# A bidirectional encoder layer on one core: the convolution is woven in denser, the backward states start among the last key sweeps, and eight instead of five steps of the recurrence stand beside the memory products

## The chip, the cores and the metric

The kernel runs on one core of a Trainium2 chip. The metric is the device time of one execution in microseconds. The time of the kernel before is the median of three runs.

## The reference, cut to what matters

One layer works on `x` of 2048 rows by 1024 columns and on 256 memory rows. A combined projection feeds two halves: a gated long convolution over 512 channels, done by transforms, and a recurrence with 4 heads in two directions (the mLSTM). Their outputs are joined and projected. A cross-attention into the memory and a feed-forward part follow.

```
u = rms_norm(x);  proj = u @ w_in                      # 1024 -> 3600 columns
hy = short_conv(proj[:, :1536])                        # z, g1, g2 of 512 columns each
for o, gate in enumerate((g1, g2)):                    # the convolution, order 2
    z = gate * (irfft(rfft(z, 2L) * spec[:, o])[:L] + z * skip[o])
q, k = silu(short_conv(proj[:, 1536:2560]));  v, o_pre, gates = proj[:, 2560:]
h = scan(q, k, v, gates[forward]) + flip(scan(flip(q), flip(k), flip(v), flip(gates[backward])))
y_ml = sigmoid(o_pre) * h                              # each scan: states C, n carried from chunk to chunk
x = x + concat(norm(z), norm(y_ml)) @ w_out
x = x + softmax(rms_norm(x) @ wq @ (memn @ wk).T) @ (memn @ wv) @ wo
x = x + relu(rms_norm(x) @ w1) ** 2 @ w2;  out = rms_norm(x)
```

## The kernel before, in words

All arithmetic is in 32-bit floats. The large products are split in a high and a low half, and each is three products of halves (lines 355, 358, 359 in `mm3`); an operand is split by a copy on ScalarE and a subtraction on VectorE (line 366).

The parts are written as Python generators. Each `yield` is a place where another part may put its instructions, and the number yielded is the weight of the step that follows. `weave(a, b, wa, wb)` advances whichever of two generators is behind in the ratio `wa` to `wb`; `among(g, h, n)` lets `h` take one step after every n-th step of `g`, and what is left of `h` at the end; `beside_each(g, h)` alternates one step of each, and `take(g, n)` hands on n steps. A scheduler then sets the final order of each engine's instructions, from this order of writing and from its own model of durations. Each engine works through its list in that order. SyncE issues most transfers and GpSimd the stores, also in order.

The parts that the change touches, by their methods of `Prog`:

- `sweep(cols, hf, first)`: a quarter of the projection's transposed columns for one half (1024) of the rows. Column pairs 0 to 5 are the convolution's three inputs, 6 and 7 are q, 8 and 9 are k. Each step is 24 products of 128x512 (`mm<-xh,wh` and so on), weight 5.5.
- `natural(hf, tiles)`: the projection's untransposed columns: tiles 0 and 1 are v, 2 and 3 the output gate, and tile 3 also the gates' columns. Each step is 4 x 24 products of 128x256 (`mm<-wh,xh`), weight 11.
- `hyena`: the convolution. For each of two orders it has three stages. The *spectrum* takes 8 blocks of z into frequency space (lines 173 and 186 with `f` as the second operand; the result is stored to `zs`). The *middle* goes over 16 blocks of frequencies (lines 956, 1030 and 987; it loads `zs` and stores `zg`). The *return* goes over 8 blocks (lines 173 and 186 with `e` as the second operand; it loads `zg`, multiplies by the gate at line 1051, and in order 1 normalises and stores `yh`). In order 0 a return block is followed by the spectrum of the next order's block.
- `gates`: small scans of the recurrence's gates over all chunks, on VectorE, with a few transposes on TensorE (lines 1093, 1134, 1149, 1171).
- `states` (through `backward` and `update`): the backward direction's state after each of chunks 15 down to 1: load `kn` and `va`, scale `va` on GpSimd (line 1196), 4 products (line 1200), 4 operations on VectorE (line 1206), store to `cbd`.
- `memproj`: the memory products. Eight weights (4 heads of keys, 4 of values): `project` (line 708), then `keys` (line 725) or `values` (line 737), each result copied by ScalarE to one of three `o` buffers (line 715) and stored by GpSimd to `gd` or `vw`.
- `mlstm`: the recurrence's outputs, 16 chunks of 128 rows. The first step loads chunks 0 and 1 and makes the scores of chunk 0. Then one step for each chunk n: scores of chunk n+1 (line 1284; exponentials on ScalarE at 1293, masks on GpSimd at 1291), outputs of chunk n in both directions (lines 1322 and 1324; the backward one reads `cbn`, loaded from `cbd`), the forward state's update (line 1200 with `ve`), and after every second chunk a normalisation (`bank_rsqrt`, lines 205 to 217, and line 1356). The scores, outputs and updates share four PSUM banks, `hy`, with the convolution.
- `attention`: the joined projection (line 1479 transposes `yh` and `ym`, products `mm<-act,wh`), then cross-attention; the remaining steps of `mlstm` are woven into it.

`program` holds the order of the whole. Its middle, as quoted below, writes in turn: the rest of the sweeps with the convolution woven in at 445 to 329; `gates` among a sweep of columns 4, 5, 8, 9 for the first half of the rows; `states` among the last natural tiles and the sweep of columns 6 and 7; then one step of `memproj`, and from there one step of `memproj` and one of `mlstm` in turn until five steps of `mlstm` (its loads, then chunks 0 to 3) are written; then `attention`.

Of the kernel before, what the change touches and what calls it, by code (L numbers as in the profile page):

```python
# [2076 lines left out]
def chain(*gens):  # L2077
    for g in gens:
        yield from g


def weave(a, b, wa, wb, until=False):
    da = db = 0.0
    fa = fb = False
    while not (fa and fb):
        if fb or (not fa and da / wa <= db / wb):
            try:
                da += next(a)
            except StopIteration:
                fa = True  # L2090
        else:
            try:
                db += next(b)
            except StopIteration:
                fb = True
                if until:
                    return


def program(p):  # L2100
    with ExitStack() as ms:
        with ExitStack() as es:
            p.inproj_open(es)
            p.filters_open()
            p.prepq = p.x_first()
            p.pop()
            s = chain(p.sweep(range(4), 0, True, lambda: p.prep_x(1)), p.opened(), p.sweep(range(4), 1, False))
            f = p.filters()
            for _ in range(5):
                next(s)  # L2110
            next(f)
            next(f)
            next(s)
            weave(s, f, 140, 102, True)
            p.gates_open(es)
            n = p.memproj()
            m = p.mlstm(ms)
            with ExitStack() as hs:
                rest = chain(s, p.sweep(range(4, 10), 1, True), p.natural(1, (3, 0, 1, 2), True),
                             p.natural(0, (3,)), among(p.sweep((4, 5, 8, 9), 0, False), p.gates(), 2),  # L2120
                             among(chain(p.natural(0, (0, 1)), p.sweep((6, 7), 0, False),
                                         p.natural(0, (2,), p.prep_mem, 2)), p.states(), 1),
                             )
                weave(rest, p.hyena(hs), 445, 329)
            for _ in chain(p.turned_in(), take(n, 1), beside_each(n, take(m, 5))):
                pass
        with ExitStack() as rs:
            p.ts = rs.enter_context(ExitStack())
            p.tail_open(p.ts)
            with ExitStack() as at:  # L2130
                g = p.attention(at)
                weave(g, m, 440, 112, True)
                ms.close()
                p.ffn_open(rs)
                for _ in g:
                    pass
            p.ffn()


def among(g, h, every):  # L2140
    for i, v in enumerate(g):
        yield v
        if i % every == every - 1:
            next(h, None)
    for _ in h:
        pass


def beside_each(g, h):
    for v in g:  # L2150
        yield v
        yield next(h, 0)
    yield from h


def take(g, n):
    for _ in range(n):
        v = next(g, None)
        if v is None:
            return  # L2160
        yield v
# [31 lines left out]
```

## Time and profile before

| | |
|---|---|
| median of the runs | 3072.69 us (3072.32 to 3078.89) |
| the profiled execution, its own time | 3076.22 us |
| its span, first to last instruction | 3074.5 us |
| TensorE (PE) busy | 2984.5 us, 97% |
| VectorE (DVE), ScalarE (ACT), GpSimd (POOL) busy | 1938.8, 1493.0, 1259.7 us |
| mean granted TensorE clock | 0.987 |
| moved by DMA | 607.03 MB, 197 GB/s |

TensorE (PE) is the engine to watch: where it is busy at full clock, other engines' waits cost nothing. Time can only be won where it stands idle or runs at a lower granted clock. Matmul records overlap (they are pipelined), so the time that a run of products takes is read from start to start. A product written once in the code stands as two records in the profile for plain 32-bit operands (lines 173, 186, 708, 725, 737, 956, 1030, 1200, 1284, 1322 and 1324), and as one for the split halves (355, 358, 359) and for transposes (825, 1479).

### The profile page before, as it was taken

To read this page: it belongs to the slowest core of one execution; us is meant where nothing else is said; L and a number is where in the kernel's file an instruction comes from. 1 tells how busy PE (TensorE), PEld (TensorE's weight loads), DVE (VectorE), ACT (ScalarE), POOL (GpSimd) and SP (SyncE) were. 2 spreads that over 40 slices of the span, in tenths; PEclk is the share of its full clock that TensorE was granted. 3 is DMA by queue.
4 is the path that set the end of the run, shared out by engine and by line. 5 is a ranking of instruction groups with operands and counts; after the bars stand their busy time and mean duration, and the time that the engine had idled before them with its cause. 6 is when DMAs were issued, how large, how long until landed. Compare 5 with 4: busy or idle time off the path is not lost.

```text
span 3074.5 us, 44129 instructions
## 1 busy us (share of the span) xinstructions
PE 2984.5 (97%) x14799; PEld 2369.8 (77%) x14799; DVE 1938.8 (63%) x3442; ACT 1493.0 (49%) x2930; POOL 1259.7 (41%) x1025
## 2 busy tenths in 40 slices
PE   9999999998999988999999999999999999999998
PEld 7666667775678757888887888888888888888876
DVE  7855454657656347867665665557555676566695
ACT  6443455635654236555544455556555543333335
POOL 0112123411344654333133247765566374344653
PEclk9999999999999988999999999999999999999999
DMA  6655687596877965464567466657544565344434
GB/s 219 196 188 171 214 271 219 184 297 200 258 223 249 349 231 192 158 220 131 188 203 259 147 210 216 208 181 243 186 154 151 195 198 171 118 158 120 155 103 164
DMA packets 423643, 607.03 MB, mean 197 GB/s; under 512 B 36846, under 2 KB 229998, under 8 KB 422392
## 3 DMA queue, kind: packets, MB, share of 16 engines
q1 hardware_dynamic: 395972, 525.42, 53.3%
q0 software_dynamic: 18992, 62.96, 5.6%
q10 hardware_dynamic: 8452, 15.83, 1.4%
q8 instruction: 117, 1.92, 0.3%
q14 instruction: 110, 0.90, 0.1%
HBM read 401.67 MB, written 202.41 MB: 196 GB/s over the span
## 4 chain that ended last, share of the span: by engine, by line
PE 58%; DVE 2%; DMA 1%; issue 1%; ACT 0%; POOL 0%; SPq 0%; DVEq 0%; ACTq 0%; POOLq 0%
PE mm L355 12%; PE mm L359 12%; PE mm L358 12%; PE hy L355 6%; PE hy L359 6%; PE hy L358 6%; PE hy L1322 1%; PE hy L1324 1%; DVE bl L1693 0%; PE hy L1284 0%; PE hy L1479 0%; PE hy L1596 0%; DVE acc L1991 0%; PE hy L1200 0%; DVE acc L2028 0%
## 5 line engine op out<-in xcount | busy, mean ns | idle before, releaser
L1692 ACT CAST ah<-w 128x512 fp32r<-128x512 f32 x284 | 176.7, 623 | 304.0 <-PE hy L358 157.8
L1693 DVE TENSOR_TENSOR bl<-wr,bh 128x512 fp32r<-128x512 f32 x213 | 235.5, 1110 | 131.1 <-ACT bh L1692 131.0
L366 DVE TENSOR_TENSOR wl<-wn,wh 128x512 fp32r<-128x512 f32 (+1 forms) x296 | 216.6, 775 | 94.3 <-ACT wh L366 94.3
L355 PE MATMUL mm<-xh,wh 128*128 128x512 f32 x640 | 263.3, 413 | 3.7 <-ACT wh L366 1.2
L358 PE MATMUL mm<-xl,wh 128*128 128x512 f32 x640 | 254.1, 397 | 4.5 <-DVE xl L366 4.4
L1692 ACT CAST bh<-wr 128x512 fp32r<-128x512 f32 x232 | 143.4, 621 | 229.0 <-PE mm L359 177.5
L359 PE MATMUL mm<-xh,wl 128*128 128x512 f32 x640 | 253.7, 397 | 0.0
L1693 DVE TENSOR_TENSOR al<-w,ah 128x512 fp32r<-128x512 f32 x236 | 213.6, 905 | 55.7 <-ACT ah L1692 55.6
L359 PE MATMUL mm<-bh,al 128*128 128x512 f32 x576 | 223.7, 391 | 4.0 <-DVE al L1693 4.0
L355 PE MATMUL mm<-bh,ah 128*128 128x512 f32 x576 | 225.8, 392 | 0.1
L358 PE MATMUL mm<-bl,ah 128*128 128x512 f32 x576 | 224.9, 390 | 0.0
L366 ACT CAST wh<-wn 128x512 fp32r<-128x512 f32 (+1 forms) x296 | 164.4, 620 | 105.8 <-PE mm L359 51.0
L358 PE MATMUL mm<-act,wh 128*128 128x512 f32 x512 | 202.0, 394 | 0.0
L355 PE MATMUL mm<-act,wh 128*128 128x512 f32 x512 | 199.4, 396 | 2.0 <-ACT wh L366 1.9
L359 PE MATMUL mm<-act,wl 128*128 128x512 f32 x512 | 199.9, 392 | 0.0
L355 PE MATMUL hy<-bh,ah 128*128 128x512 f32 x448 | 175.2, 391 | 0.0
L358 PE MATMUL hy<-bl,ah 128*128 128x512 f32 x448 | 174.6, 390 | 0.0
L359 PE MATMUL hy<-bh,al 128*128 128x512 f32 x448 | 174.4, 390 | 0.0
L331 POOL TENSOR_TENSOR b<-b 128x512 f32<-128x512 f32 x32 | 48.1, 1505 | 294.6 <-DVE b L330 275.2
L355 PEld LDWEIGHTS mm<-xh,wh 128*128 128x128 f32 x640 | 120.5, 188 | 53.1 <-issue 19.4
L358 PEld LDWEIGHTS mm<-xl,wh 128*128 128x128 f32 x640 | 120.6, 188 | 49.2 <-issue 18.6
L355 PE MATMUL mm<-wh,xh 128*128 128x256 f32 (+1 forms) x512 | 154.7, 302 | 0.0
(396 smaller groups left out, 8262.9 us busy)
## 6 DMA issues: line engine op xcount, KB each, us to landing
wr<-hc SPq DMA_DIRECT2D x224, 256.0 KB
w<-in_ff_w_dram SPq DMA_DIRECT2D x172, 256.0 KB
hc<-wn SPq DMA_DIRECT2D x128, 256.0 KB
wn<-in_w_in_dram SPq DMA_DIRECT2D x100, 256.0 KB
hc<-q SPq DMA_DIRECT2D x96, 256.0 KB
fs<-a SPq DMA_DIRECT2D x32, 512.0 KB
zs<-a POOLq DMA_DIRECT2D x32, 512.0 KB, 6.0
a<-fs SPq DMA_DIRECT2D x64, 256.0 KB
```

What stands on the lines that cost most here:

```text
L331: nc.gpsimd.tensor_tensor(b, f, b, ALU.subtract)
L355: first = mm(ps, lh, rh, start=start, stop=False)
L358: mm(ps, lh, rl, start=False, stop=False)
L359: self.last = mm(ps, ll, rh, start=False, stop=stop)
L366: both = (self.nc.scalar.copy(hi, src), self.nc.vector.tensor_tensor(lo, src, hi.bitcast(F32), ALU.subtract))
L1322: nc.tensor.matmul(dst, nm[:, h], va[:, h], start=True, stop=state is None)
L1324: nc.tensor.matmul(dst, rows_[d, 1][:, h], state[:, h], start=False, stop=True)
L1692: self.nc.scalar.copy(hi, src)
L1693: eng.tensor_tensor(lo, src, hi.bitcast(F32), ALU.subtract)
```

## The change

The order in `program` is changed; no instruction's work is.

```
-                             p.natural(0, (3,)), among(p.sweep((4, 5, 8, 9), 0, False), p.gates(), 2),
-                             among(chain(p.natural(0, (0, 1)), p.sweep((6, 7), 0, False),
-                                         p.natural(0, (2,), p.prep_mem, 2)), p.states(), 1),
+                             p.natural(0, (3,)),
+                             paced(chain(p.sweep((4, 5, 8, 9), 0, False), p.natural(0, (0, 1))),
+                                   p.gates(), back := p.states(), (0, 1) * 6 + (2,) * 6 + (2, 0)),
+                             among(chain(p.sweep((6, 7), 0, False), p.natural(0, (2,), p.prep_mem, 2)), back, 1),
                              )
-                weave(rest, p.hyena(hs), 445, 329)
-            for _ in chain(p.turned_in(), take(n, 1), beside_each(n, take(m, 5))):
+                weave(rest, p.hyena(hs), 400, 329)
+            for _ in chain(p.turned_in(), take(n, 1), beside_each(n, take(m, 8))):
                 pass
+def paced(g, h1, h2, plan):
+    for v, n in zip(g, plan):
+        yield v
+        if n:
+            next((h1, h2)[n - 1], None)
+    yield from g
```

- The weave of projection and convolution goes from 445:329 to 400:329, so that the convolution advances faster against the projection and is written to its end when the projection has some 45 units of weight left.
- `paced` takes the steps of `gates` after every second one of the first 12 steps of the sweep of columns 4, 5, 8 and 9, as before, and then 7 steps of `states` after the sweep's last four steps and the first three of the v tiles. Before, `states` began with the v tiles. The rest of `states` goes among the sweep of columns 6 and 7 and the last output-gate tile.
- Eight steps of `mlstm` (the loads, then chunks 0 to 6) are written beside the memory products and right after them, where five were.

How the scheduler then placed things, at three places. First TensorE's list at the end of the memory products, before. L708 and L737 are memory products, L173 and L186 with `e` the convolution's return, L1284 scores of the recurrence, L1322 and L1324 its outputs.

```order
L708 MATMUL mm<-mt,wm 128x256 x6
L173 MATMUL hy<-a,e_2743 32x512
L186 MATMUL hy<-a,e_2743 32x512 x7
L708 MATMUL mm<-mt,wm 128x256 x10
L737 MATMUL mm<-wm,kt 128x512 x10
L1284 MATMUL hy<-qn,kk_t 128x128 x8
L737 MATMUL mm<-wm,kt 128x512 x6
L1322 MATMUL hy<-va,rw 128x129 x5
L1324 MATMUL hy<-cbn,rw 128x129
```

And the place in the changed kernel where the recurrence's first chunk begins; L725 is a memory product of the keys, L1200 with `va` a backward state.

```order
L725 MATMUL mm<-kt,wm 128x256 x16
L1200 MATMUL hy<-va,kn 128x129 x8
L708 MATMUL mm<-mt,wm 128x256 x7
L1284 MATMUL hy<-qn,kk_t 128x128 x8
L708 MATMUL mm<-mt,wm 128x256 x9
L725 MATMUL mm<-kt,wm 128x256
L1322 MATMUL hy<-va,rw 128x129 x6
L725 MATMUL mm<-kt,wm 128x256 x12
L1324 MATMUL hy<-cbn,rw 128x129
```

Before, the last memory product stands ahead of the first output of chunk 0, and the scores of chunk 0 and 1 stand six products ahead of it. Now 57 products of line 708, 16 of line 725 and 32 of line 737 stand behind those scores, and outputs of chunks 0 to 4 stand among them. The last two backward states stand seven products ahead of the scores.

Second, TensorE's list at the end of the memory products in the changed kernel (the scores here are those of chunk 6, the outputs those of chunk 5):

```order
L737 MATMUL mm<-wm,kt 128x512 x3
L1200 MATMUL hy<-ve,kn 128x129 x4
L737 MATMUL mm<-wm,kt 128x512 x3
L1284 MATMUL hy<-qn,kk_t 128x128 x4
L1322 MATMUL hy<-va,rw 128x129
L1324 MATMUL hy<-cf,rw 128x129
L1322 MATMUL hy<-va,rw 128x129
```

Behind the last memory product stand the outputs of chunks 5 and 6 (16 products each) with their updates, and then 16 transposes of line 1479. Before, it was the outputs of chunks 0 to 3, and then the same transposes.

Third, TensorE's list where order 1 of the convolution goes from the spectrum to the middle. Before, 24 sweep products, 4 transposes (L825) and small ones stand between the last spectrum block (L173, L186 with `f`) and the first product of the middle on it (L1030); this is the end of that piece:

```order
L355 MATMUL mm<-xh,wh 128x512
L358 MATMUL mm<-xl,wh 128x512
L359 MATMUL mm<-xh,wl 128x512
L825 MATMUL mm<-ident,cv 128x128 x4
L1030 MATMUL hy<-a,dm 128x512 x2
```

Now 9 sweep products and the pair of line 956 stand there:

```order
L186 MATMUL hy<-a,f_104 64x512 x7
L355 MATMUL mm<-xh,wh 128x512
L358 MATMUL mm<-xl,wh 128x512
L359 MATMUL mm<-xh,wl 128x512
L355 MATMUL mm<-xh,wh 128x512
L358 MATMUL mm<-xl,wh 128x512
L359 MATMUL mm<-xh,wl 128x512
L355 MATMUL mm<-xh,wh 128x512
L358 MATMUL mm<-xl,wh 128x512
L359 MATMUL mm<-xh,wl 128x512
L956 MATMUL mm<-a,dm 128x512 x2
L1030 MATMUL hy<-a,dm 128x512 x2
```

So the first product on the last spectrum block moved nearer to it. The transposes of `gates` (L1093, L1134, L1149, L1171) moved too: before they stand among the return and spectrum blocks of order 0, now all of them stand in the middle of order 1.

On TensorE's list two return blocks of order 1 stand among the memory products now, where six stood, and five updates of `states` stand there, where six stood. On SyncE's list the first loads of the joined projection's weights now stand ahead of twelve transfers of memory weights, and their first waits for the convolution's last stores; before, the first load with such a wait (`wn<-yh`) stood behind the last memory weight.

## The prediction, made before the changed kernel had run

> **What bounds the kernel now.** I read the page first, then the busy time by stretches, then TensorE's timeline where it is idle, then the waits.
>
> ```profile
> PE 2984.5 (97%) x14799; PEld 2369.8 (77%) x14799; DVE 1938.8 (63%) x3442; ACT 1493.0 (49%) x2930; POOL 1259.7 (41%) x1025
> ...
> PE   9999999998999988999999999999999999999998
> ...
> PEclk9999999999999988999999999999999999999999
> ```
>
> TensorE (PE) is busy for 97% of the span, so only 90 us of idle time and some time at a low clock can be had at all. The change adds no work to PE. What it can move is where PE waits.
>
> The stretches of 75 us show where (columns: busy time of PE, PEld, DVE, ACT, POOL; granted clock; DMA share; GB/s):
>
> ```profile
> 675.00:750.00 75.00, 64.67 (x370) 41.35 (x369) 55.14 (x173) 32.73 (x57) 9.46 (x15) 0.93 0.70 231
> ...
> 975.00:1050.00 75.00, 72.69 (x427) 61.38 (x426) 34.62 (x102) 21.14 (x51) 47.15 (x56) 0.98 1.02 347
> ...
> 1125.00:1200.00 75.00, 54.27 (x309) 49.07 (x310) 49.79 (x165) 40.78 (x156) 32.66 (x29) 0.80 0.63 208
> 1200.00:1275.00 75.00, 75.00 (x392) 64.15 (x392) 61.74 (x155) 44.59 (x129) 30.65 (x24) 1.00 0.50 155
> ```
>
> The worst stretch, 1125 to 1200 us, has 20.7 us of idle time and a clock of 0.80. It is the place that the last part of the change is about. The second worst, 675 to 750 us, is the return of order 0 with `gates` on top. In the next stretch PE is full, with the recurrence woven into the attention.
>
> PE's timeline through the worst stretch:
>
> ```profile
> 1116.84 5.32 PE L737 MATMUL mm<-wm,kt 128*128 128x512 f32 x12
> 1121.99 1.28 PE L1322 MATMUL hy<-va,rw 128*128 128x129 f32 x10
> ...
> 1126.80 1.16 PE L1284 MATMUL hy<-qn,kk_t 128*128 128x128 f32 x8
> 1127.80 0.39 PE L1322 MATMUL hy<-va,rw 128*128 128x129 f32 x2
> 1128.02 0.39 PE L1324 MATMUL hy<-cf,rw 128*128 128x129 f32 x2
> ...
> 1135.22 0.67 PE L1322 MATMUL hy<-va,rw 128*128 128x129 f32 x2 [4.58 <-DVE den L1330]
> ...
> 1139.83 1.16 PE L1284 MATMUL hy<-qn,kk_t 128*128 128x128 f32 x8 [0.93 <-DVE cf L1206]
> ...
> 1158.80 1.92 PE L1284 MATMUL hy<-qn,kk_t 128*128 128x128 f32 x8
> ...
> 1165.63 1.23 PE L1200 MATMUL hy<-ve,kn 128*128 128x129 f32 x8 [0.36 <-ACT ht L1336]
> ...
> 1174.90 1.12 PE L1479 MATMUL hy<-ident,wn 128*128 128x128 f32 x4 [5.17 <-DVE act L366]
> ...
> 1179.10 1.49 PE L355 MATMUL mm<-act,wh 128*128 128x512 f32 x4
> ...
> 1194.11 1.91 PE L1479 MATMUL hy<-ident,wn 128*128 128x128 f32 x16
> ```
> ```profile
> 1140.00:1150.00 10.00, 4.92 (x25) 4.49 (x26) 6.58 (x22) 4.12 (x20) 1.73 (x2) 0.61 0.40 109
> 1150.00:1160.00 10.00, 7.07 (x30) 6.48 (x31) 7.87 (x31) 4.74 (x18) 7.31 (x7) 0.50 0.28 105
> ```
>
> The last memory product's run ends at 1121.99. From there to the first product of the joined projection at 1179.10, PE has only the recurrence: outputs of chunks 0 to 3, one chunk waiting for the other through ScalarE, VectorE and GpSimd. I call such chunks bare. That is 57.1 us, part of it at half clock, as the two stretches of 10 us show.
>
> **Term 1, the bare chunks.** A chunk's content at full clock: scores 1.0 us (1126.80 to 1127.80), outputs 16 products at 0.22 us (a row of two records follows the other after 0.22), 3.6 us, update about 1.0: 5.6 us. In the 57.1 us there are 64 output products (12 + 3 x 16 + 4: 14.3 us), four updates (4), four scores (4) and the 16 transposes (1.9, as at 1194.11): 24.2 us. So 32.9 us are lost. In the changed list two chunks are bare, 5 and 6: 36 output products (8.1), two updates, three scores and the transposes: 15 us. How long they take I read from the old ones. From scores to scores, or to the update's end, chunk 1 took 13.0 us (1126.80 to 1139.83), chunk 2, behind the normalisation of the pair before, 19.0 (to 1158.80), chunk 3 8.1 (to 1166.86). Chunk 5 is like 1 and 3, taken as 10; chunk 6 is like 2, taken as 17, since the clock was already halved when chunk 2 began. The tail from there to the first product was 12.2 us; 5.2 of it is a wait for VectorE, busy with a normalisation that will not stand there (the next comes after chunk 7), so 8. That gives 35 us instead of 57.1: 22.1 us shorter, of which 9.2 is content that goes elsewhere. Gain 12.9, between 3.7 (13, 19 and 12.2: 44.2 us) and 17.8 (8.1, 15 and 7: 30.1 us).
>
> **Term 2, the chunks beside the memory.** The moved content costs what it costs; the question is waits. Prices of the memory products and the waits among them now:
>
> ```profile
> 1041.74 5.45 PE L725 MATMUL mm<-kt,wm 128*128 128x256 f32 x24
> ...
> 1047.02 7.07 PE L708 MATMUL mm<-mt,wm 128*128 128x256 f32 x32
> ...
> 1106.47 8.75 PE L737 MATMUL mm<-wm,kt 128*128 128x512 f32 x20
> ```
> ```profile
> 1011.66 3.03 PE L725 MATMUL mm<-kt,wm 128*128 128x256 f32 x8 [2.31 <-ACT kt L710]
> 1086.33 1.16 PE L1200 MATMUL hy<-va,kn 128*128 128x129 f32 x8 [2.94 <-POOL va L1196]
> ```
>
> The waits among them are 5.3 us. A product of line 708 or 725 takes 0.44 us, one of 737 0.875. So from scores to scores the list now gives chunks 1 to 4 18.6, 14.6, 19.4 and 14.2 us (their own 5.6 and 9, 14 and 10 memory products or the like). Against their own pace of 8 to 19 us that is just enough for odd ones, and short by a little for chunk 4 and its like. I take 4 us of waits over the four chunks (0 where the pace at full clock is shorter, 12 where each waits 3). Chunk 0 needs the last backward state: store to `cbd`, then load `cbn`.
>
> ```profile
> L1206 DVE SCALAR_TENSOR_TENSOR cb<-cb,cols,hy x56: 336/342/352, 872.1 to 1087.9; 128x129 f32<-128x129 f32 x56
> ```
> ```profile
> cbd<-cb POOLq DMA_DIRECT2D x6, 258.0 KB, 7.9
> ```
>
> From the last two updates, which stand together: eight operations of VectorE 2.7, 7.9 from issue to landing (the median over 985 to 1125 us), a load of 3.4 like that of `zs` under term 3: 14.0 us. The list has 7 products, 8 scores, 9 + 1 products and 4 outputs in between: 17 x 0.44 + 1.9 + 0.9 = 10.3. So a wait of 3.7, less if the transfers are lighter loaded. Six return blocks leave this stretch with their loads, where the DMA share is 1.02 now; that relieves it. Sum 7.7 against 5.3: a loss of 2.4 (bounds: a gain of 3, a loss of 12).
>
> **Term 3, the denser convolution.** The price of sweep products and of the pair of line 956, and the passage from spectrum to middle of order 1 before:
>
> ```profile
> 406.99 0.39 PE L358 MATMUL mm<-xl,wh 128*128 128x512 f32 x1
> 407.22 0.40 PE L359 MATMUL mm<-xh,wl 128*128 128x512 f32 x1
> 407.45 1.88 PE L956 MATMUL mm<-a,dm 128*128 128x512 f32 x4
> ...
> 728.88 0.63 PE L186 MATMUL hy<-a,f 32*64 32x512 f32 x7
> ...
> 731.04 1.05 POOL L339 DMA_DIRECT2D zs<-a  x2 [2.47 <-ACT st L201]
> ...
> 736.26 1.16 SPq L920 DMA_DIRECT2D a<-zs  x2
> ...
> 739.70 2.90 PE L1030 MATMUL hy<-a,dm 128*128 128x512 f32 x3 [3.62 <-DMA a<-zs]
> ```
>
> From the last block's end at 729.5 it takes 10.2 us through GpSimd, a store and a load, and 3.6 of it is a wait. The cover goes from 24 sweep products and transposes to 9 products at 0.23 (2.1) and the pair of line 956 (1.9): 4.0 us. The wait becomes 6.2, a loss of 2.6. The list also has spectrum and return blocks back to back at three places, where the banks have to be copied out first; I take 0.5 each, 1.5 (0 to 5.4, at the 1.81 of the row at 714.81 below). In return, `gates` leaves order 0's return, where PE waits:
>
> ```profile
> 705.97 0.64 PE L173 MATMUL hy<-a,f 32*64 32x512 f32 x1 [1.30 <-DVE a L1051]
> 712.62 0.37 PE L1134 MATMUL hy<-ident,ends 128*1 128x128 f32 x1 [2.70 <-DVE ends L1129]
> 714.81 1.03 PE L173 MATMUL hy<-a,e 64*32 64x512 f32 x1 [1.81 <-issue]
> ```
>
> These 5.8 us go, but the same scans now load VectorE in the middle of order 1. I keep 4 of them: gain 1.8. Sum: a loss of 2.3 (bounds: a gain of 3, where the new place hides the scans and the blocks cost nothing; a loss of 9, where it hides none and VectorE's 5.8 us come a second time).
>
> The attention loses three chunks from its cover; PE was full in 1200 to 1275 us with them, so nothing. `states` starts four sweep steps earlier; its products waited for no one there, nothing.
>
> **Sum.** -12.9 + 2.4 + 2.3 = -8.2 us. The profiled execution took 3076.22 us (span 3074.5), 3.5 above the median of the runs; from it 3068.0 would follow, from the median, against which the result is measured, 3064.5.
>
> The Trainium skill, "TensorE: Matmul & The Clock Gate", section "HAM oscillation — how this bites in real kernels", says that an idle gap of TensorE of more than about 3.4 us halves its clock. The trace agrees: rows of line 1322 take 0.39 us before the wait of 4.58 and 0.67 behind it. By this rule the waits of 3.7 and 6.2 above would each be followed by a window at half clock, an estimate of 1.7 us each from the page's figure; the sum would be -4.8, 3067.9 us.
>
> **Rivals.**
>
> A is the forecast: two bare chunks less, part of it given back in waits. 3060 to 3070.
>
> B: the chunks beside the memory wait for nothing new (the store of `cbd` lands in time, because the transfers are relieved), and the denser convolution costs nothing net. For it speaks that in 1200 to 1275 us such chunks cause no idle time at all; against it, that they have far more cover there. -12.9 - 3 + 0 = -15.9, 3056.8.
>
> C: the denser convolution takes the gain back. Where VectorE is late in the middle of order 1, PE waits at each of its 16 blocks; at the bound of 9 us, with term 2 as above, it is -1.5: 3071.2.
>
> D, slower: ScalarE's queue. The copies of memory results (line 715) wait there for one of three buffers, until its store has landed:
>
> ```profile
> ACT o L715 <- DMA gd<-o: 27.6, 9, 8.5
> ...
> ACT o L715 <- DMA vw<-o: 7.2, 3, 4.2
> ```
>
> That is 34.8 us in which ScalarE's list stands still. It costs little now, because next to nothing of the recurrence stands behind them. In the changed list the exponentials, output scalings and update scalings of chunks 0 to 6 do. If half of it reaches PE, 17.4 us come on top: +9.2, 3081.9. Against it speaks that fewer other transfers compete, so stores land sooner. It decides the sign when more than 8.2 of the 34.8 us reach PE. The Trainium skill, "TensorE: Matmul & The Clock Gate", section "Architectural detail: the array is 16× 32×32, not 1× 128×128", calls ScalarE's and VectorE's queues strictly first in, first out; that is the rule by which nothing could overtake such a copy.
>
> **How the numbers follow.** A 0.40, B 0.25, C 0.18, D 0.17. About 0.2%, 6 us, is what a measurement of this kernel tells from no change. A lies across that bound and counts 0.25 as faster, 0.15 as the same; B is faster, C the same, D slower but for 0.02. Faster 0.50, same 0.35, slower 0.15. The range 3051 to 3079 holds A, C, nearly all of B and the milder cases of D, some 0.85.
>
> **What would show it.** Right: between the last memory product and the first product of the joined projection some 35 us instead of 57; a clock near 0.9 over those 75 us; outputs of chunk 0 to 4 among the memory products with one wait of 3 to 6 us before the first backward output; a wait of about 6 us at line 1030 where order 1's middle starts. Wrong: waits of line 1322 for ScalarE among the memory products that add up to more than 10 us, or 715 waiting as long as now (D); line 1134 waiting over 5 us (C); the bare stretch still over 45 us, which would take away the gain.

## The result and the profile after

| | before | after |
|---|---|---|
| median of the runs | 3072.51 us (3071.01 to 3078.89) | 3090.55 us (3087.36 to 3097.53) |
| ratio to before, 95% interval | | 1.0058 (1.0035 to 1.0081) |
| the profiled execution, span | 3074.5 us | 3090.8 us |
| first memory product (line 708) | 988.1 us | 1033.2 us |
| first product of the joined projection | 1179.1 us | 1209.6 us |
| from there to the end | 1895.4 us | 1881.2 us |

The changed kernel is slower by about 18 us; 8 us less had been forecast. In the two spans the difference is 16.3 us: 45.1 us lost up to the first memory product, 14.6 won from there to the joined projection, 14.2 won behind it.

The page's lines for TensorE (PE), after:

```profile
PE 2984.9 (97%) x14799; PEld 2367.8 (77%) x14799; DVE 1954.6 (63%) x3442; ACT 1494.0 (48%) x2930; POOL 1263.6 (41%) x1025
...
PE   9999999988999998999999999999999999999998
...
PEclk9999999999999998999999999999999999999999
```

The work is the same. In the rows by tenths the dent behind the memory (slices 15 and 16 before) is down to slice 16, and the one in slice 10 (692 to 769 us before) now takes slices 9 and 10 (618 to 773 us). The stretches that the prediction showed, after (columns as there):

```profile
675.00:750.00 75.00, 64.24 (x327) 40.69 (x326) 36.73 (x63) 32.70 (x56) 13.84 (x17) 0.95 0.70 216
...
975.00:1050.00 75.00, 75.00 (x485) 63.94 (x484) 57.65 (x126) 30.32 (x53) 44.24 (x49) 1.00 0.81 259
...
1125.00:1200.00 75.00, 66.87 (x352) 50.57 (x351) 42.48 (x162) 37.74 (x144) 39.87 (x43) 0.96 0.67 223
1200.00:1275.00 75.00, 70.75 (x383) 61.88 (x382) 59.54 (x133) 44.59 (x129) 32.24 (x25) 0.93 0.62 195
```

1125 to 1200 us had 54.27 us of work at a clock of 0.80. That place is mended. Where the time went is seen in four stretches ahead of the memory, first before, then after:

```profile
340.00:400.00 60.00, 56.28 (x336) 39.86 (x333) 25.46 (x39) 27.25 (x41) 7.84 (x13) 1.00 0.86 298
400.00:530.00 130.00, 125.03 (x634) 89.49 (x634) 76.69 (x121) 82.35 (x142) 38.90 (x44) 0.99 0.72 229
600.00:750.00 150.00, 137.26 (x878) 98.55 (x877) 100.83 (x249) 63.92 (x111) 28.46 (x36) 0.97 0.76 245
750.00:900.00 150.00, 147.81 (x726) 104.53 (x725) 95.84 (x151) 99.44 (x174) 59.86 (x65) 1.00 0.77 237
```
```profile
340.00:400.00 60.00, 48.85 (x291) 32.43 (x291) 25.45 (x38) 26.84 (x41) 8.89 (x15) 0.89 0.87 284
400.00:530.00 130.00, 122.54 (x535) 83.54 (x534) 76.65 (x123) 81.52 (x139) 38.49 (x42) 0.99 0.74 231
600.00:750.00 150.00, 132.31 (x903) 96.96 (x902) 77.03 (x134) 59.23 (x105) 28.39 (x39) 0.98 0.81 252
750.00:900.00 150.00, 133.03 (x486) 82.89 (x486) 121.58 (x263) 99.87 (x168) 55.18 (x57) 0.95 0.71 217
```

PE's idle time grows by 7.4, 2.5, 5.0 and 14.8 us, 29.7 in all. In the two stretches whose clock fell, that costs another 0.11 x 60 + 0.05 x 150 = 14 us, as an estimate. Two places carry it: the convolution's first blocks (340 to 400), and the middle of its order 1 (750 to 900), where VectorE's busy time rises from 95.84 to 121.58 us.

At the first place PE's waits, before and then after, with one block that waits for nothing:

```profile
352.01 0.64 PE L173 MATMUL hy<-z,f 32*64 32x512 f32 x1 [1.10 <-ACT a L311]
...
360.08 0.61 PE L173 MATMUL hy<-z,f 32*64 32x512 f32 x1 [1.17 <-ACT a L998]
...
381.86 0.61 PE L173 MATMUL hy<-a,f 32*64 32x512 f32 x1 [1.45 <-DMA a<-hy]
```
```profile
346.57 0.64 PE L173 MATMUL hy<-z,f 32*64 32x512 f32 x1 [2.69 <-ACT a L311]
...
379.88 1.08 PE L173 MATMUL hy<-a,f 32*64 32x512 f32 x1 [4.73 <-DMA a<-hy]
...
389.03 0.64 PE L173 MATMUL hy<-a,f 32*64 32x512 f32 x1
...
389.51 0.63 PE L186 MATMUL hy<-a,f 32*64 32x512 f32 x7
...
393.84 0.64 PE L173 MATMUL hy<-a,f 32*64 32x512 f32 x1 [3.70 <-ACT a L998]
```

3.7 us of waits became 11.1. A block, 16 records, takes 1.1 us (389.03 to 390.14); behind the long wait a record of line 173 takes 1.08 instead of 0.64.

At the second place, the convolution's largest wait for VectorE, and VectorE's own list ahead of its end:

```profile
774.64 2.04 PE L956 MATMUL mm<-a,dm 128*128 128x512 f32 x2 [7.13 <-DVE a L960]
```
```profile
769.38 0.27 DVE L1114 TENSOR_TENSOR pad<-pad 64x128 f32<-64x128 f32 x1
769.69 0.29 DVE L1115 TENSOR_TENSOR pad<-pad 64x128 f32<-64x128 f32 x1
...
771.59 0.29 DVE L1115 TENSOR_TENSOR pad<-pad 64x128 f32<-64x128 f32 x1
...
772.27 0.69 DVE L1034 TENSOR_TENSOR b<-hy,a 128x512 f32<-128x512 f32 x1
772.99 0.69 DVE L959 COPY a<-mm 64x512 f32<-64x512 f32 x1
773.70 0.69 DVE L960 COPY a<-mm 64x512 f32<-64x512 f32 x1
```

The copy that frees the bank for line 956 (773.70) stands behind the doubling steps of `gates` (lines 1114 and 1115). VectorE works through its list in order and is busy for 19.48 of the 20 us from 770 to 790. The scans are not all that it does there: copies and products of the middle (lines 959, 960, 1034) stand among them.

Behind the memory, PE's timeline where the prediction priced chunks 5 and 6:

```profile
1176.95 2.74 PE L737 MATMUL mm<-wm,kt 128*128 128x512 f32 x6
1179.53 1.05 PE L1284 MATMUL hy<-qn,kk_t 128*128 128x128 f32 x8
...
1186.45 1.16 PE L1284 MATMUL hy<-qn,kk_t 128*128 128x128 f32 x8 [0.70 <-DVE cf L1206]
...
1195.71 0.77 PE L1322 MATMUL hy<-va,rw 128*128 128x129 f32 x2 [6.26 <-DVE bry L213]
1196.27 0.64 PE L1324 MATMUL hy<-cbn,rw 128*128 128x129 f32 x2
...
1204.67 3.35 PE L1479 MATMUL hy<-ident,wn 128*128 128x128 f32 x16
...
1209.57 0.71 PE L355 MATMUL mm<-act,wh 128*128 128x512 f32 x2
```

From the last memory product (1179.7) to the joined projection it is 29.9 us, where it was 56.9 with four bare chunks.

### The profile page after: what moved, and what is told of

Same layout as the page of the kernel before. It is cut to its first block, busy times and chain, and to the rows that moved or that the text cites. A ratio compares the mean times of both kernels' runs of the same rounds, so it can differ in the third digit from the quotient of the medians.

```text
span 3090.8 us, 44177 instructions
## 1 busy us (share of the span) xinstructions
PE 2984.9 (97%) x14799; PEld 2367.8 (77%) x14799; DVE 1954.6 (63%) x3442; ACT 1494.0 (48%) x2930; POOL 1263.6 (41%) x1025
## 4 chain that ended last, share of the span: by engine, by line
PE 54%; DVE 2%; DMA 2%; issue 1%; POOL 1%; ACT 0%; SPq 0%; DVEq 0%; ACTq 0%; POOLq 0%
PE mm L355 12%; PE mm L359 12%; PE mm L358 12%; PE hy L359 6%; PE hy L355 6%; PE hy L358 6%; DMA w<-in_ff_w_dram 1%; PE hy L1322 0%; PE hy L1324 0%; PE hy L1479 0%; DVE bl L1693 0%; DVE al L1693 0%; DMA h<-acc 0%; PE hy L1596 0%; DVE acc L1991 0%
## 5 line engine op out<-in xcount | busy, mean ns | idle before, releaser
L1522 POOL TENSOR_TENSOR ssum<-ssum,sq 128x512 f32<-128x512 f32 x56 | 81.2, 1450 | 200.9 <-ACT sq L1521 191.8
```

Of the source, the lines that this page charges most:

```text
L1522: nc.gpsimd.tensor_tensor(ssum, ssum, sq, ALU.add)
```

## The experiments

Fifteen kernels were run. The table puts them side by side: the ratio to before, the first memory product, the time from there to the joined projection, how much of that is the bare stretch (from the last memory product) with how many chunks wholly in it by TensorE's list, and the rest to the end. The last four columns are of the profiled execution, a single one, whose time lies up to 5 us beside the median of its kernel (e14 5.4 below, e19 4.6 above), so that a few us between two rows of them say little.

| kernel | ratio (95% interval) | first memory product, us | to the joined projection | bare stretch (chunks) | rest |
|---|---|---|---|---|---|
| before | 1 | 988.1 | 191.0 | 56.9 (4) | 1895.4 |
| after | 1.0058 (1.0035 to 1.0081) | 1033.2 | 176.4 | 29.9 (2) | 1881.2 |
| e1 ratio only | 1.0083 (1.0068 to 1.0099) | 1035.6 | 170.6 | 32.7 (2) | 1891.0 |
| e7 eight steps only | 1.0067 (1.0052 to 1.0083) | 989.3 | 224.0 | 93.3 (7) | 1875.4 |
| e10 earlier states only | 0.9969 (0.9958 to 0.9980) | 998.0 | 173.6 | 38.5 (2) | 1890.4 |
| e2 after, ratio undone | 1.0033 (1.0020 to 1.0045) | 998.7 | 209.1 | 76.5 (5) | 1874.2 |
| e14 after, five steps | 1.0026 (1.0014 to 1.0037) | 1030.4 | 152.1 | 11.1 (0) | 1889.1 |
| e3 after, scans cut | 1.0040 (1.0025 to 1.0055) | 1031.3 | 177.0 | 31.1 (2) | 1874.3 |
| e4 after, later start | 1.0027 (1.0014 to 1.0039) | 1008.7 | 191.7 | 55.2 (4) | 1874.3 |
| e21 e4 and old middle | 1.0068 (1.0054 to 1.0082) | 1004.5 | 213.8 | 71.6 (5) | 1873.2 |
| e23 e21, scans cut | 1.0054 (1.0040 to 1.0069) | 995.0 | 212.1 | 70.5 (5) | 1875.4 |
| e16 e10, scans later | 0.9983 (0.9971 to 0.9994) | 1001.3 | 172.2 | 38.6 (2) | 1889.0 |
| e11 e10, order 1 at 1/0.72 | 0.9998 (0.9985 to 1.0011) | 1015.3 | 163.4 | 23.6 (1) | 1889.9 |
| e12 e10, order 1 at 1/0.85 | 0.9959 (0.9946 to 0.9971) | 1001.2 | 160.8 | 25.9 (2) | 1890.8 |
| e19 e12, old passage | 0.9955 (0.9942 to 0.9969) | 1002.3 | 166.3 | 26.9 (2) | 1888.9 |
| e13 e10, closer return | 0.9972 (0.9961 to 0.9984) | 992.3 | 175.3 | 37.6 (2) | 1891.6 |
| e18 e13, weight ahead of the middle | 0.9982 (0.9973 to 0.9992) | 996.0 | 178.1 | 35.4 (2) | 1890.6 |

Behind the first memory product still stand 2 to 6 return blocks (1.1 us each) and 3 to 9 backward states (1.2 us each), by kernel; between two kernels that makes up to 6 us of content. A hundredth of a per cent of the ratio is 0.3 us.

**The three parts apart.** Theory T, after the traces were compared: the denser convolution costs what was lost ahead of the memory, and the other parts are innocent of it.

e1, on the kernel before:

```
-                weave(rest, p.hyena(hs), 445, 329)
+                weave(rest, p.hyena(hs), 400, 329)
```

> The kernel before with the ratio 400:329 alone. Theory T (the denser convolution itself costs the time: it starts earlier in the first sweeps, its blocks stand back to back, and the gates' scans fall beside order 1's middle): the first memory product starts 35 to 45 us later than before, the bare stretch behind the memory shortens by 10 to 20 us (some five chunks, two or three of them bare), and the time is 3085 to 3100 us. Rival T3 (the earlier backward states cost it): the way to the first memory product loses under 15 us, and the time is 3050 to 3070.

3098.12 us: the first memory product 47.5 us late, bare stretch 24.2 us shorter. T holds, though both lie above its ranges (35 to 45 and 10 to 20), and T3 falls.

e2, on the changed kernel:

```
-                weave(rest, p.hyena(hs), 400, 329)
+                weave(rest, p.hyena(hs), 445, 329)
```

> The changed kernel with the ratio back at 445:329, so that earlier states and eight steps of the recurrence stay. Theory T: the way to the first memory product is as long as before within 6 us, and four or five chunks are bare again at some 8 us of loss each, so 3070 to 3085 us. Rival T3 (the earlier states): at least 20 of the 39 us on the way to the memory stay lost, and the time is 3090 to 3110.

3081.89 us, the first memory product at 998.7 (10.6 late, of which three more states are 3.5, so that T's 6 us are passed by one), five chunks bare: T. Against the changed kernel the way to the memory is 34.5 us shorter, the stretch behind it 32.7 longer and the rest 7.0 shorter; by the ratios 7.7 us are won, with intervals that overlap. So the ratio makes the memory late, but with eight steps written most of what its undoing wins there is lost again in the bare stretch.

e7, on the kernel before:

```
-            for _ in chain(p.turned_in(), take(n, 1), beside_each(n, take(m, 5))):
+            for _ in chain(p.turned_in(), take(n, 1), beside_each(n, take(m, 8))):
```

> The kernel before with eight steps of the recurrence instead of five, alone. Six chunks are bare. Theory T: nothing is lost up to the memory; the three chunks more cost what a bare chunk loses (32.9 us in four, 8 each) and the attention saves nothing by them, so 3072 + 24 = 3090 to 3100 us. Rival T4 (chunks that leave the attention give their waits back there): 3065 to 3080.

3092.05 us: in T's range. Seven chunks are bare, where six were expected, and a pair of them takes 25 us from scores to scores, in a rhythm of waits for VectorE and half-clocked rows:

```profile
1165.45 1.16 PE L1284 MATMUL hy<-qn,kk_t 128*128 128x128 f32 x8 [0.70 <-DVE cf L1206]
...
1173.42 0.77 PE L1322 MATMUL hy<-va,rw 128*128 128x129 f32 x2 [4.97 <-DVE bry L213]
...
1190.41 1.16 PE L1284 MATMUL hy<-qn,kk_t 128*128 128x128 f32 x8 [0.70 <-DVE cf L1206]
```

The table gives a chunk's two prices. Bare: (93.3 - 11.1) / 7 = 11.7 us, and the stretches with 1, 2, 4 and 5 chunks lie within 9 us of that line. In the attention: the rest takes 1889 to 1895 us with five steps and 1873 to 1881 with eight, some 15 us for three chunks, 5 each, which is their content. T's word that the attention saves nothing by them was wrong in this: it saves the content, and the 33 us of e7's longer stretch outweigh it.

e10, on the kernel before, takes `paced` alone (445:329 and five steps stay):

```
-                             p.natural(0, (3,)), among(p.sweep((4, 5, 8, 9), 0, False), p.gates(), 2),
+                             p.natural(0, (3,)),
+                             paced(chain(p.sweep((4, 5, 8, 9), 0, False), p.natural(0, (0, 1))),
+                                   p.gates(), back := p.states(), (0, 1) * 6 + (2,) * 6 + (2, 0)),
...
```

> The kernel before with the earlier backward states alone (ratio 445:329, five steps). Theory T (the ratio costs the time, the bare chunks beyond cover cost the rest): the way to the first memory product stays within 4 us of before at equal content, two chunks come among the memory products, and two instead of four are bare, 3058 to 3068 us. Rival T3 (earlier states cost time in order 1's middle): 3076 to 3090.

3060.69 us. Two chunks come among the memory products and two stay bare, as T had it; the way to the memory is 9.9 us longer, of which three more states are 3.5, so the "within 4 us" is missed by some 2. Of the three parts this is the only one that gains alone.

e14, on the changed kernel:

```
-            for _ in chain(p.turned_in(), take(n, 1), beside_each(n, take(m, 8))):
+            for _ in chain(p.turned_in(), take(n, 1), beside_each(n, take(m, 5))):
```

> The changed kernel with five steps of the recurrence beside the memory instead of eight; all four chunks of them stand among the memory products, none is bare. Theory T (the loss lies ahead of the memory, 39 us, and a bare chunk costs some 5 us more than one in the attention): the way to the first memory product as in the changed kernel, the bare stretch under 12 us, 3074 to 3084 us. Rival T4 (chunks beside the memory are worth it where the convolution has ended): 3090 to 3100.

3078.66 us, no chunk bare. TensorE at the end of the memory:

```profile
1159.68 11.75 PE L737 MATMUL mm<-wm,kt 128*128 128x512 f32 x27
1174.38 1.09 PE L1479 MATMUL hy<-ident,wn 128*128 128x128 f32 x4 [2.95 <-DMA wn<-yh]
...
1182.54 1.18 PE L355 MATMUL mm<-act,wh 128*128 128x512 f32 x4
```

So the three more chunks make the changed kernel slower, by 10 us from the two ratios. In the profiled executions it is 24.3 us more from the first memory product to the joined projection and 8 less behind it (15 to 20 in the other kernels with eight steps), 16 us; e14's execution lies 5.4 us under its median and the changed kernel's 2 above. e1 and e14 differ by the earlier states alone (-17.5 us), e10 and e14 by the ratio alone (+17.5 us). The three parts do not add: alone they make +25.5 (ratio), +20.6 (eight steps) and -9.5 us (earlier states), together +17.8.

**Where the ratio costs.** e4, on the changed kernel, puts the convolution's first block where it stood:

```
-        yield 52
+        yield 58
```

> The changed kernel with the convolution's first block put 6 units of weight later, where it stands before; its density, the gates and the eight steps stay. Theory T: the waits between 340 and 530 us fall back by 10 to 15 us; the convolution ends later too, so some four chunks are bare instead of two (8 to 15 us back): 3083 to 3093 us, with the first memory product 10 to 15 us earlier than in the changed kernel at equal content. Rival T2 (the ratio, not the start, crowds the transfers of the first spectrum): the waits between 340 and 530 us stay within 4 us of the changed kernel's, and the time is 3095 to 3105.

3078.18 us. Its row of the first stretch and its waits there are those of before:

```profile
340.00:400.00 60.00, 55.95 (x343) 38.20 (x342) 26.85 (x41) 28.36 (x43) 8.49 (x15) 1.00 0.86 294
```
```profile
353.06 0.64 PE L173 MATMUL hy<-z,f 32*64 32x512 f32 x1 [1.10 <-ACT a L311]
...
361.13 0.61 PE L173 MATMUL hy<-z,f 32*64 32x512 f32 x1 [1.17 <-ACT a L998]
...
383.26 0.61 PE L173 MATMUL hy<-a,f 32*64 32x512 f32 x1 [1.78 <-DVE wl L366]
```

The waits follow the start, not the density; T2 falls at this place. The first memory product comes 24.5 us earlier, of which 2 is content, more than T's 10 to 15 and more than the first stretch explains (7 us of idle time, and 0.11 of the clock over 60 us): order 1's middle improves too (140.11 us of work in 750 to 900 us, clock 0.98, against 133.03 and 0.95), since all of it meets another part of the sweeps. The wait of 7.13 us at line 956 is gone too, although the scans still stand beside the middle. 15.3 us of this are given back, with four chunks bare again; the time lies 5 us under T's range.

e3, on the changed kernel, cuts VectorE's scans in `gates`:

```
-                s = 1
+                s = 64
...
-            nc.vector.memset(mm[:, 0, 0, 0], 0.0)
-            nc.vector.memset(mm[:, 0, 1, 15], 0.0)
-            for s in range(16):
+            nc.vector.memset(mm, 0.0)
+            for s in range(1):
```

> The changed kernel with the gates' scans cut: of the doubling steps only the last is done, and of the chain over 16 chunks only the first link, so that their VectorE work (some 40 us) falls away and the result of the recurrence is another one. Theory T, with VectorE's scans in order 1's middle as the larger part: the waits at 774 (7.1 us) and the low clock behind it go, 15 to 22 us less than the changed kernel, 3068 to 3076 us. Rival T2 (transfers, which the denser convolution crowds, cost the time: waits for hy, fs, zs, zg): under 6 us less, 3084 to 3091.

3083.44 us, 5.5 us less by the ratios: the wait of 7.13 us is gone, and 750 to 900 us hold 140.13 us of work instead of 133.03. But the first memory product is only 1.9 us earlier, since the scheduler also set other products differently in the sweeps and a wait of 5.9 us stands near 350 us there. T's 15 to 22 us did not come: the gain is in T2's "under 6", the time 0.6 us under its range, and the intervals of the two ratios overlap. So nothing here shows the scans as the larger part of the loss.

e16, on e10, moves the scans into order 1's middle at the old density:

```
-                                   p.gates(), back := p.states(), (0, 1) * 6 + (2,) * 6 + (2, 0)),
+                                   p.gates(), back := p.states(), (0,) * 6 + (1,) * 6 + (2,) * 6 + (2, 0)),
```

> The kernel with the earlier backward states alone, but the six steps of the gates stand after the second six sweep steps instead of after every second one, so that their scans fall into order 1's middle at its old density. Theory T (the scans on VectorE in the middle cost): a wait of 4 us or more for VectorE at line 956 in the middle, 3066 to 3076 us against 3061. Rival T5 (only the middle's density costs): 3058 to 3064.

3065.01 us against 3060.69, 4.3 us by the ratios, with overlapping intervals; the time lies between T's range and T5's. The waits are there, but at the gates' own lines, not at 956:

```profile
735.24 0.37 PE L1134 MATMUL hy<-ident,ends 128*1 128x128 f32 x1 [4.00 <-DVE ends L1129]
...
769.52 0.26 PE L1149 MATMUL hy<-ident,mm 1*128 1x1 f32 x1 [3.50 <-DVE mm L1144]
```

e11 and e12, on e10, let order 1 alone go faster (0.72, then 0.85):

```
+        pace = (1.0, 0.72)
-            yield 4
+            yield 4 * pace[o]
-                yield 4.6
+                yield 4.6 * pace[o]
-            yield 5
+            yield 5 * pace[o]
-                yield 4.5 if o else 6.0
+                yield 4.5 * pace[o] if o else 6.0
```

> Ratio 445:329, but order 1 of the convolution goes 1/0.72 times as fast, so that it too ends ahead of the projection; everything up to order 1's middle stands as before, the gates' scans included; five steps. Theory T with the loss in the places (start in the first sweeps; scans on VectorE in order 1's middle): only the middle's own density costs, under 12 us, the bare stretch has two chunks, 3058 to 3070 us. Rival T5 (a denser middle costs by itself what it cost in the changed kernel, some 20 us, whatever the scans do): 3074 to 3088.

3069.99 us, at the upper end of T's range. The scans stand where they did before, and still the way to the memory is 17.3 us longer than in e10, more than T's 12. At the passage from spectrum to middle (line 1031 here, 1030 before) and in the middle:

```profile
743.98 3.75 PE L1031 MATMUL hy<-a,dm 128*128 128x512 f32 x4 [7.52 <-DMA a<-zs]
```
```profile
750.00:900.00 150.00, 138.70 (x578) 89.61 (x577) 101.00 (x165) 95.17 (x162) 59.61 (x67) 0.97 0.79 239
```

> As the kernel with order 1 at 1/0.72, with 1/0.85. Theory T: nearly no loss in the middle, two or three bare chunks, 3054 to 3066 us, no slower than the denser one. T5: half its loss, 3066 to 3076, faster than the denser one by 8 or more.

3056.02 us, 14 less than at 0.72. The first memory product is only 3.2 us later than in e10 and the bare stretch 12.6 shorter. By these two points the loss grows faster than the density: T was right at 0.85; at 0.72 the loss on the way is near T5's 20 us, the time T's.

e19, on e12, restores the list at the passage:

```
-            yield 4 * pace[o]
+            yield (4, 5)[o]
```

> The kernel with order 1 at 1/0.85, but the weight of the passage from spectrum to middle set to 5, so that the list there is the one of before (24 sweep products between the last spectrum block and line 1030's first product). If the uncovered passage is a price of its own: the wait of 7.35 us at line 1030 falls to 3 to 4 us, the clock there rises from 0.74 to about 0.9, and the time is 3 to 8 us less, 3046 to 3056. If not: 3053 to 3062.

3054.62 us, the same as e12 within the intervals. The wait at line 1031 falls from 7.35 to 3.69 us and the clock in 730 to 750 us rises from 0.74 to 0.83, but the first memory product comes no earlier: in 810 to 850 us the idle time goes from 4.2 to 6.1 us and the clock from 0.96 to 0.91. The time fits both alternatives. No price of the uncovered passage is seen, but the intervals, some 5 us together, do not exclude one of the size that was expected.

e13, on e10, closes up only the return of order 1; e18 goes on from it (0.5) and raises the weight ahead of the middle:

```
-            yield 5
+            yield (5, 3)[o]
-                yield 4.5 if o else 6.0
+                yield 2.7 if o else 6.0
```
```
-            yield 4
+            yield (4, 9)[o]
```

> The kernel before with the earlier backward states and, of the convolution, only order 1's return closer (weights times 0.6, ratio 445:329), five steps: start, gates and order 1's middle stand as before, and the convolution ends earlier all the same. Theory T' (what costs is the crowding in order 1's middle and at the start, not the return's): the first memory product comes within 5 us of the kernel with earlier states alone, two chunks are bare or fewer, 3048 to 3058 us. Rival T6 (the return's blocks, closer together, wait for their loads and for VectorE): 3060 to 3068.

3061.90 us, as e10: the way to the memory is 5.7 us shorter, of which one more state behind it is 1.2, the stretch behind 1.7 longer, and still two chunks are bare. The number is T6's, the waits are not found; the closer return neither helps nor harms.

> As the kernel with a closer return (times 0.5 here), and the weight ahead of order 1's middle goes from 4 to 9, so that a full sweep step more stands between the last spectrum block and the middle. If the wait at line 1030 there (3.6 us before, 4.4 to 7.5 where the passage was crowded) and the low clock behind it are a price of their own: that wait falls under 1 us and the time is 3 to 8 us under the kernel with a closer return alone, 3043 to 3055 us. If the rest of the middle only moves its waits elsewhere: the same as that kernel or up to 6 us slower.

3066.14 us. This decides nothing: the scheduler set line 1030's product at the same place as before (24 sweep products ahead of it), and its wait is 3.70 us.

**Do the places add up?** e21, on the changed kernel, undoes the start and the density of order 1's middle; e23 cuts the scans besides, as in e3:

```
-        yield 52
+        yield 58
-            yield 4
+            yield (4, 4.45)[o]
-                yield 4.6
+                yield (4.6, 5.12)[o]
```

> The changed kernel with two parts of the denser convolution undone: its first block 6 units later, and order 1's middle at its old density (its weights times 445/400). Order 0 stays denser, the gates' scans stay beside the middle, eight steps. If the middle's density is a price of its own: the first memory product comes 8 to 20 us earlier than with the later start alone (1019.7 us), near 1005, and no wait for fs or zs over 2 us is left between 825 and 900 us; 3066 to 3080 us with three chunks bare. If the middle's loss in the changed kernel was the scans alone: 1014 to 1022 us, with the waits for VectorE at line 956 as large as there, 3076 to 3090.

The 1019.7 us in this expectation is not e4's figure; that is 1008.7. Against that, e21's 1004.5 is 4.2 earlier, 1 of it content: at the changed kernel's ratio the middle's density alone costs little, so the first alternative fails; a wait for fs of 3.9 us is left too. Of the second alternative's signs, the waits for VectorE at line 956 are not there. The time, 3093.19 us, fits neither: what was won ahead of the memory was lost behind it. By TensorE's list the convolution's last return block stands among the first products of line 737 (1086.45 us), where in e4 it stands among those of line 725 (1058.39), and five chunks are bare.

> The kernel with both parts undone, and the gates' scans cut (of the doubling steps only the last, of the chain only its first link; the recurrence's result is another one). If the scans are a price of 5 to 10 us of their own: the waits for VectorE among the first half of order 1's middle go, and the time is 5 to 10 us under that kernel. If their price came only together with the dense middle: within 3 us of it.

3085.45 us; the first memory product is 9.5 us earlier, the time 4.3 less by the ratios, between the two expectations. With e3 (5.5 us for cutting the scans) and e16 (4.3 for moving them there), three comparisons point to a price of 4 to 6 us for the scans beside the middle. None of them is clear of its uncertainty, which by the intervals is 5 to 8 us each.

## Why the prediction was wrong

- **The step that failed is term 3, the denser convolution**: a loss of 2.3 us, bounds up to 9. Measured, the way to the memory is 45.1 us longer. Four return blocks and one state more stand on it (4 x 1.1 + 1.2 = 5.6), so 39.5 us were lost. That the ratio costs it is shown (e1, e2). Three things in the term:
  - It has no entry for the first blocks, which start 6 units of weight earlier beside the first sweeps. Waits there rose by 7.4 us and the clock fell to 0.89; with the start moved back (e4) both went, and 22 us of the 39.5. Some 14 of these lie in this stretch (7.1 of idle time and 0.11 x 60 of clock); the others go mostly in order 1's middle.
  - For the scans it wrote down a gain of 1.8 us, which supposed that the middle hides most of them. The runs point to 4 to 6 us of loss instead, not clear of noise. At line 1134, where the waits were looked for, there was none; VectorE's list delayed the copy at line 960 instead, and that wait is gone where the start is later (e4).
  - The blocks' crowding was priced from single waits of before, 1.5 us. The waits also lower the clock and come several times over in the middle: 14.8 us of idle time in 750 to 900 us. How much of these is the denser middle and how much its meeting other sweep steps is not settled: e21 and e12 put the first at little, e11 at much.
- **Term 1** was at the edge of its bounds: 29.9 us, where 35 were taken and 30.1 was the least. The stretch is 27.0 us shorter, 9.2 of it content: a gain of 17.8, not 12.9. Chunk 5 took 6.9 us (10 taken), chunk 6 18.2 (17), the tail 4.9 (8).
- **Term 2** was a gain, not a loss. Of PE's waits for others among the memory products only one is left; no output waits for `cbn`:

```profile
1055.58 1.99 PE L725 MATMUL mm<-kt,wm 128*128 128x256 f32 x8 [2.03 <-ACT kt L710]
```

  From the first memory product to the joined projection 14.6 us were won, although three chunks more and 5.6 us of blocks and states less stand there (16.8 - 5.6 = 11.2): 25.8 us of waits and low clock went, where terms 1 and 2 gave 10.5. 17.8 are term 1's, so term 2 gained 8.0 where it had put down a loss of 2.4.
- **The chunks that leave the attention** were priced at nothing, and 14.2 us came back against 16.8 of content. That was near; the other kernels with eight steps have only 1873 to 1875 us there. What the sum never asked is whether five steps would have done: with five, this list has no bare chunk at all (e14), and eight cost 10 us.
- **Rival C** had one of the mechanisms, VectorE late in order 1's middle, and was bounded at 9 us from the waits of before (term 3's own entries would give 2.6 + 1.5 + 5.8 = 9.9). **Rival D** is out; of the 34.8 us in which ScalarE's list stood still, 10.9 are left (2.4 for `vw`), and no output waits for ScalarE among the memory products:

```profile
ACT o L715 <- DMA gd<-o: 8.5, 3, 5.3
```

- **The signs.** 29.9 us instead of 35 behind the memory, a clock of 0.96 instead of 0.9, and 4.4 us instead of 6 at line 1030 came; the wait of 3 to 6 us before the first backward output did not. The signs watched only places that the sum named, and the larger loss was at ones that it did not name.
- **The second estimate**, -4.8 us, counted its two windows of 1.7 us whole. At half clock only half of a window is lost, which gives -6.5; it would not have changed the forecast.

The sum as measured in the spans: 39.5 - 25.8 + 2.6 = +16.3 us.

## What to carry to other kernels

A weave's ratio moves everything behind it, its start too: price each stage of the woven part against what it will now stand beside, not only the end that the ratio is meant to move. Price dependent work by where it stands (here 11.7 us a chunk bare, 5 under cover), and move no more of it than the cover takes. Where a change has several parts, run each alone: here one gained 9.5 us, the others lost 21 and 25, and the best version (e19, or e12, at 0.9955 and 0.9959) keeps the one that gains and speeds up only the last order by a little.

## What was not expected of the hardware

The clock stays low for longer than the wait that lowered it. Behind the 6.26 us at 1195.71 rows of line 1324 take 0.64 us instead of 0.39, and the 16 transposes at 1204.67 still take 3.35 instead of the 1.91 of before; two stretches of 10 us, after:

```profile
1190.00:1200.00 10.00, 3.48 (x14) 3.21 (x15) 6.88 (x28) 2.70 (x15) 1.50 (x3) 0.70 0.36 110
1200.00:1210.00 10.00, 7.87 (x46) 7.53 (x45) 7.17 (x22) 8.61 (x31) 5.81 (x5) 0.62 0.57 177
```

That is some 12 us at half clock, with only short waits (0.81 and 2.13 us) in between. The last of them ends at 1202.80, and 6 us later a row of line 1322 takes 0.39 us again:

```profile
1202.80 2.09 PE L1200 MATMUL hy<-ve,kn 128*128 128x129 f32 x8 [2.13 <-ACT ht L1336]
...
1208.76 0.39 PE L1322 MATMUL hy<-va,rw 128*128 128x129 f32 x2
```

The Trainium skill, "TensorE: Matmul & The Clock Gate", section "HAM oscillation — how this bites in real kernels", gives about 1.67 us of throttled time after each such wait in the kernel that it describes, whose bursts of products between two waits last about 2 us. The prediction took that figure over as a price for any wait, and here the measurement is several times as long.
